# Mixer steps of a hybrid trunk: one place per unit of the dense stream instead of four

## The chip, the cores and the metric

The kernel runs on one core of a Trainium2 chip. The metric is the device time of one execution in microseconds, the median of several runs. Names of engines: TensorE (PE, with its weight loads PEld), VectorE (DVE), ScalarE (ACT), GpSimd (POOL) and SyncE (SP), which issues most of the DMAs.

## The reference

One pre-norm residual layer and a final norm on 256 tokens of width 2048, all in float32:

```python
D_MODEL = 2048; SEQ = 256; DEPTH = 1
h = rms_norm(x, norm_w)
p = h @ w_in                       # 2048 x 16592, one combined projection
qkv, z, b, a, feat, rz, su, sz, gates = split(p)
y0 = gated_delta_net(silu(conv4(qkv)), b, a) ; y0 = rms_norm(y0) * silu(z)   # 8 heads of 128, chunks
y1 = rwkv7(shift_mix(feat))                  ; y1 = (layer_norm(y1) + bonus) * silu(rz)  # 16 heads of 64
y2 = s5(su)                                  ; y2 = glu(gelu(y2)) * silu(sz) # 64 groups x 64 states
m  = sum(sigmoid(gates[i] + gate_b[i]) * (y[i] @ w_branch[i]) for i in range(3))
x  = x + m @ w_out
out = rms_norm(x, final_norm_w)
```

By far the largest part of the arithmetic is dense: w_in, w_branch, the glu weight and w_out. The three token mixers are many small matmuls with short elementwise chains between them.

## The kernel before

**The dense stream.** All dense work is one stream of *units*. A unit is 1024 columns' worth of weight, loaded by DMA as one 512 KB tile `raw` (four buffers), and split into a high part `whi` on ACT (L279) and a rest `wlo` on DVE (L280) two units ahead of its use (`load_unit`, called by `run_stream`). PE then does 24 matmuls of a full unit: for each of 8 slices of 128 rows high by high, high by low and low by high, into a bank of PSUM. A *job* is 128 output columns: 16 slices in two units for w_in, 8 slices in one unit for w_branch and the glu weight. When a job ends, `done` takes the result out of PSUM: a conv (ACT L665, then three DVE L667) for q, k, v of the delta net, a token shift (ACT L440, DVE L441) for r, k, v of the RWKV part, and a gate (`silu2`: ACT L684, DVE L685) for gz and rz. Two PSUM banks, `mm`, serve the dense jobs in turn; six, `br`, the mixers.

**The front** has eight rounds of eight jobs each (q, k, v, gz, r, k, v, rz), then gate jobs and the columns of S5. The tiles `gz` and `rz` have two buffers each, which become free again where the mixer's last step uses them: L821 for gz, behind the transposes `gp`, and the end of `rwkv_tail` for rz, behind the transposes `rq`. **The back** has the projections of the branches and the gates, with the S5 mixer beside it, the glu, and w_out.

**Mixer work** is written as generators. Each does a piece of work, a *step*, and yields how many calls of `pump` it wants to wait till its next one. They stand in queues called lanes: b (decays), g and r (the front parts of a delta-net head and an RWKV pair), t and i (the triangular inverses), g2 and r2 (their tails), s and sm (S5's tiles and S5's matrices). `pump()` counts each lane's `due` down and runs a step of those that are due. Before, it is called four times in a unit of eight slices: behind slices 1, 3 and 5 and after the unit, and a lane runs steps until it is no longer due.

**What sets the order.** PE's order is the program's: the class `InOrder` chains every matmul to the one before it. So a mixer matmul whose input isn't ready holds up the dense matmuls that are written behind it. The order on DVE, ACT and POOL comes from a scheduler that works from the program and the dependencies.

Names in the rows below: `gn` (norm sums of a head), `gp` and `rq` (the closing transposes of a head, of a pair), `ra`, `rc`, `rd`, `re` (RWKV state steps), `g` (delta-net tail), `ivp`/`ivZ` (the inverse on DVE, L548 and L550), `sm` (small columns: rsqrt chains at L121 to L137), `s5u`, `s5y` (S5 inputs and outputs of a tile), `s5wt`, `s5bt`, `s5ct` (its matrices).

Of the kernel before, what the change touches and what calls it, by code (L numbers as in the profile page):

```python
# [36 lines left out]
def tile_trunk(  # L37
# [1035 lines left out]
    lanes = {}  # L1073
    due = {}

    def lane(name, gen):
        lanes.setdefault(name, deque()).append(gen)

    def pump():
        for name in list(lanes):  # L1080
            due[name] = due.get(name, 0) - 1 if lanes[name] else 0
            while lanes[name] and due[name] <= 0:
                due[name] += step(name)

    def step(name):
        q = lanes[name]
        while q:
            try:
                return next(q[0])
            except StopIteration:  # L1090
                q.popleft()
        due[name] = 0
        return 0
# [11 lines left out]
    def mm_unit(u):  # L1105
        job = u["job"]
        if u["k0"] == 0:
            job["ps"] = [(br_bank if job["nps"] > 1 else mm_bank)(f"mm{un[0]}_{j}") for j in range(job["nps"])]
        kt, w, k0 = u["kt"], u["w"], u["k0"]
        last = k0 + kt == job["K"]  # L1110
        mh, ml = job["mov"]()
        if job["tok"]:

            job.setdefault("units", []).append(u)
            todo = [(0, u), (1, u)]
            if job["late"]:
                todo = [(0, u)] + [(1, v) for v in job["units"] if last]
            for a, v in todo:
                o = job["ps"][a]
                for k in range(kt):  # L1120
                    kk = v["k0"] + k
                    end = kk == job["K"] - 1
                    mhs, mls = mh[:, kk, a * P:(a + 1) * P], ml[:, kk, a * P:(a + 1) * P]
                    pe.matmul(o[:, 0:w], lhsT=mhs, rhs=v["hi"][:, k], start=kk == 0, stop=False)
                    pe.matmul(o[:, 0:w], lhsT=mhs, rhs=v["lo"][:, k], start=False, stop=False)
                    pe.matmul(o[:, 0:w], lhsT=mls, rhs=v["hi"][:, k], start=False, stop=end)
                if end:
                    job["done"](a, o)
        else:
            for k in range(kt):  # L1130
                kk = k0 + k
                if "pre" in job:
                    job["pre"](kk)
                for j, (c0, c1) in enumerate(job["cuts"]):
                    o = job["ps"][j][0:c1 - c0, 0:T]
                    pe.matmul(o, lhsT=u["hi"][:, k, c0:c1], rhs=mh[:, kk], start=kk == 0, stop=False)
                    pe.matmul(o, lhsT=u["hi"][:, k, c0:c1], rhs=ml[:, kk], start=False, stop=False)
                    pe.matmul(o, lhsT=u["lo"][:, k, c0:c1], rhs=mh[:, kk], start=False,
                              stop=last and k == kt - 1)
                if k % 2 and k < kt - 1:  # L1140
                    pump()
        if last and not job["tok"]:
            job["done"](job["ps"])
            if "after" in job:
                job["after"]()
# [36 lines left out]
    def run_stream(gen, ahead=2, q=()):  # L1182
        q = deque(q)
        gen = iter(gen)
        done = False
        while True:
            while not done and len(q) < ahead:
                try:
                    u = next(gen)
                except StopIteration:  # L1190
                    done = True
                    break
                load_unit(u)
                q.append(u)
            if not q:
                return
            mm_unit(q.popleft())
            pump()
# [528 lines left out]
```

## Time and profile before

| what | value |
|---|---|
| median of 3 runs | 1205.7 us (1205.07 to 1205.96) |
| profiled execution, its own time | 1205.63 us |
| its span in the profile | 1203.9 us |
| PE busy | 1181.4 us, 98% |
| DVE busy | 960.6 us, 80% |
| ACT busy | 621.1 us, 52% |
| HBM read | 195.88 MB |
| bytes moved over the span | 169 GB/s |

The time of an execution is a little more than the span, which goes from the first to the last record. Busy shares are averages over stages: the rounds of the front and their tails last to the last L821 at 614.5 us, S5's tiles fall into about 690 to 935 us, and the 260 us after that are dense work alone. Rows of groups read: line, engine, operation, output<-inputs, shape, count, then busy us and mean ns of one, then the idle time of the engine just ahead of them. Rows of the timeline read: start in us, length in us, engine, line, operation. A matmul of mixer data in float32 appears as two records.

### The profile page before, as it was taken

To read this page: it belongs to the slowest core of one execution; us is meant where nothing else is said; L and a number is where in the kernel's file an instruction comes from. 1 tells how busy PE (TensorE), PEld (TensorE's weight loads), DVE (VectorE), ACT (ScalarE), POOL (GpSimd) and SP (SyncE) were. 2 spreads that over 40 slices of the span, in tenths; PEclk is the share of its full clock that TensorE was granted. 3 is DMA by queue.
4 is the path that set the end of the run, shared out by engine and by line. 5 is a ranking of instruction groups with operands and counts; after the bars stand their busy time and mean duration, and the time that the engine had idled before them with its cause. 6 is when DMAs were issued, how large, how long until landed. Compare 5 with 4: busy or idle time off the path is not lost. (4 is left out here: it accounts for less than half of the span.)

```text
span 1203.9 us, 29305 instructions
## 1 busy us (share of the span) xinstructions
PE 1181.4 (98%) x11658; PEld 1127.5 (94%) x11658; DVE 960.6 (80%) x2515; ACT 621.1 (52%) x1190; POOL 62.9 (5%) x96
## 2 busy tenths in 40 slices
PE   5999999999999999999999999999999999999997
PEld 5999999999999999999999999999999999999886
DVE  7869888989899898977558988999998765555555
ACT  5455555556555656564544554444443554444443
POOL 4000000000000000000002011111100000000000
PEclk8999999999999999999999999999999999999999
DMA  5776655555555555555557677666767667677763
GB/s 167 196 192 156 167 129 157 138 150 144 136 150 141 146 145 147 134 141 142 158 163 194 191 193 185 184 183 187 195 170 196 171 181 189 179 190 238 240 197 115
DMA packets 384643, 203.98 MB, mean 169 GB/s; under 512 B 38825, under 2 KB 376186, under 8 KB 384122
## 3 DMA queue, kind: packets, MB, share of 16 engines
q1 hardware_dynamic: 382650, 199.61, 61.0%
q0 software_dynamic: 1536, 1.58, 0.5%
q8 instruction: 92, 1.51, 0.5%
q10 hardware_dynamic: 320, 0.93, 0.2%
q14 instruction: 45, 0.37, 0.1%
HBM read 195.88 MB, written 6.18 MB: 168 GB/s over the span
## 5 line engine op out<-in xcount | busy, mean ns | idle before, releaser
L62 PE MATMUL mm<-hT,whi 128*128 128x256 f32 (+1 forms) x4160 | 784.0, 289 | 4.2 <-DVE hT L247 3.5
L62 PEld LDWEIGHTS mm<-hT,whi 128*128 128x128 f32 (+1 forms) x4160 | 646.3, 191 | 17.8 <-DVE hT L247 4.3
L62 PE MATMUL mm<-hT,wlo 128*128 128x256 f32 (+1 forms) x2080 | 588.4, 283 | 0.4 <-DVE wlo L280 0.4
L279 ACT ACTIVATE whi<-raw 128x1024 fp32r<-128x1024 f32 (+1 forms) x346 | 364.6, 1055 | 361.1 <-PE mm L62 289.0
L280 DVE TENSOR_TENSOR wlo<-raw,whi 128x1024 fp32r<-128x1024 f32 (+1 forms) x345 | 422.2, 1224 | 151.0 <-ACT whi L279 149.2
L62 PEld LDWEIGHTS mm<-hT,wlo 128*128 128x128 f32 (+1 forms) x2080 | 397.4, 191 | 0.6 <-DVE wlo L280 0.6
L62 PE MATMUL mm<-oT,whi 128*128 128x256 f32 x768 | 140.4, 283 | 0.0
L62 PEld LDWEIGHTS mm<-oT,whi 128*128 128x128 f32 x768 | 118.9, 190 | 0.4 <-issue 0.4
L62 PE MATMUL mm<-oT,wlo 128*128 128x256 f32 x384 | 108.4, 282 | 0.0
L62 PE MATMUL mm<-whi,mT 128*128 128x512 f32 (+1 forms) x288 | 76.9, 354 | 0.0
L62 PEld LDWEIGHTS mm<-oT,wlo 128*128 128x128 f32 x384 | 73.2, 191 | 0.2 <-DVE wlo L280 0.2
L62 PEld LDWEIGHTS mm<-whi,mT 128*128 128x128 f32 x288 | 51.2, 189 | 7.5
L62 PE MATMUL mm<-wlo,mT 128*128 128x512 f32 (+1 forms) x144 | 50.9, 354 | 0.0
L548 DVE TENSOR_TENSOR ivp<-ivZ,ivX 48x1 f32<-48x1 f32 (+14 forms) x120 | 34.4, 287 | 1.4
L667 DVE SCALAR_TENSOR_TENSOR gc<-mm,pv,gc 128x255 f32<-128x255 f32 (+2 forms) x72 | 34.1, 473 | 0.9 <-ACT gc L665 0.3
L62 PEld LDWEIGHTS mm<-wlo,mT 128*128 128x128 f32 x144 | 27.2, 189 | 3.7
L550 DVE TENSOR_REDUCE ivZ<-ivp 48x1 f32<-48x1 f32 (+14 forms) x120 | 27.2, 227 | 1.5
L62 PE MATMUL mm<-ysp,whi 128*128 128x256 f32 x128 | 22.8, 281 | 0.0
L1220 DVE SCALAR_TENSOR_TENSOR gate<-gate,mm 128x256 f32<-128x256 f32 x32 | 13.4, 418 | 11.4 <-PE mm L62 11.4
L1210 ACT ACTIVATE gate<-mm,hgate 128x256 f32<-128x256 f32 x48 | 22.1, 461 | 0.3
L62 PEld LDWEIGHTS mm<-ysp,whi 128*128 128x128 f32 x128 | 19.6, 188 | 0.0
L670 ACT ACTIVATE gth<-gc 128x256 f32<-128x256 f32 x24 | 9.8, 410 | 16.6 <-DVE gc L667 15.1
(541 smaller groups left out, 1266.7 us busy)
## 6 DMA issues: line engine op xcount, KB each, us to landing
raw<-in_w_in_dram SPq DMA_DIRECT2D x256, 512.0 KB
raw<-in_w_branch_dram SPq DMA_DIRECT2D x48, 512.0 KB
raw<-in_w_out_dram SPq DMA_DIRECT2D x32, 512.0 KB
raw<-in_s_glu_w_dram SPq DMA_DIRECT2D x8, 512.0 KB
xs<-in_x_dram SPq DMA_DIRECT2D x4, 512.0 KB
xr<-in_x_dram SPq DMA_DIRECT2D x2, 1024.0 KB
raw<-in_w_in_dram SPq DMA_DIRECT2D x4, 384.0 KB
gr<-grow SPq DMA_DIRECT2D x8, 128.0 KB
```

Of the source, the lines that this page charges most:

```text
L62: return self.put(nc.tensor.matmul(*a, **k).ins)
L279: u["top"] = lambda: se.activation(out=hi[:, 0:nn], in_=raw[:, 0:nn], func=AF.Copy)
L280: u["sub"] = lambda eng=ve: eng.tensor_tensor(out=lo[:, 0:nn], in0=raw[:, 0:nn], in1=hi[:, 0:nn].bitcast(F32), op=ALU.subtract)
L548: ve.tensor_tensor(out=pi, in0=Z[:, 0:i, 0:i].rearrange("p j c -> p c j"), in1=X[:, i, 0:i].unsqueeze(1).to_broadcast([8 * NU, i, i]), op= ...
L550: ve.tensor_reduce(out=Z[:, i, 0:i], in_=pi, axis=AX.X, op=ALU.add)
L667: ve.scalar_tensor_tensor(out=c[:, s:T], in0=p[:, 0:T - s], scalar=pv("cw", (3 - s) * 24 + col), in1=c[:, s:T], op0=ALU.mult, op1=ALU.add)
L670: se.activation(out=th, in_=c, func=AF.Tanh, scale=0.5)
L1210: se.activation(out=t, in_=pss[0][:, 0:T], func=AF.Tanh, scale=0.5, bias=hgate[:, b * 16 + i:b * 16 + i + 1])
L1220: ve.scalar_tensor_tensor(out=g, in0=g, scalar=1.0, in1=p0, op0=ALU.add, op1=ALU.mult)
```

## The change

`pump()` is called only after a unit, no longer behind slices 1, 3 and 5. Each call takes 4 from `due`, so that the yields keep their meaning. A lane that is due does one step and then stops; a `due` below zero stays and lets the lane run a step at the next place too. The lanes s and sm still run steps until they are no longer due.

```diff
--- before.py
+++ after.py
@@ -1076,11 +1076,17 @@
     def lane(name, gen):
         lanes.setdefault(name, deque()).append(gen)
 
+    SLOT = 4
+    RUNS = ("s", "sm")
+
     def pump():
+
         for name in list(lanes):
-            due[name] = due.get(name, 0) - 1 if lanes[name] else 0
+            due[name] = due.get(name, 0) - SLOT if lanes[name] else 0
             while lanes[name] and due[name] <= 0:
                 due[name] += step(name)
+                if name not in RUNS:
+                    break
 
     def step(name):
         q = lanes[name]
@@ -1137,8 +1143,6 @@
                     pe.matmul(o, lhsT=u["hi"][:, k, c0:c1], rhs=ml[:, kk], start=False, stop=False)
                     pe.matmul(o, lhsT=u["lo"][:, k, c0:c1], rhs=mh[:, kk], start=False,
                               stop=last and k == kt - 1)
-                if k % 2 and k < kt - 1:
-                    pump()
         if last and not job["tok"]:
             job["done"](job["ps"])
             if "after" in job:
```

The number of instructions on each engine stays as it was. Dense matmuls on PE are interrupted by mixer matmuls at 162 places where there were 236. Lines behind the first hunk move by 6, those behind the second by 4.

PE, the closing transposes `gp` of head 1. Before, they stand alone in the midst of a unit (unit 60.5 counted in dense matmuls):

```order
L62 MATMUL mm_0_3534<-hT_75,whi_3441 128x256
L62 MATMUL mm_0_3534<-hT_76,whi_3441 128x256
L62 MATMUL mm_0_3534<-hT_75,wlo_3442 128x256
L65 MATMUL gp_3559<-ident,got_3308 128x128 x2
L62 MATMUL mm_0_3534<-hT_75,whi_3441 128x256
L62 MATMUL mm_0_3534<-hT_76,whi_3441 128x256
L62 MATMUL mm_0_3534<-hT_75,wlo_3442 128x256
```

With the change they come after unit 62, behind `gn` and `ra` of other lanes:

```order
L62 MATMUL mm_0_3519<-hT_75,wlo_3516 128x256
L62 MATMUL gn_3614<-ones,gsq_3488 128x1 x2
...
L62 MATMUL ra_3631<-rUV_3433,rg_3244 64x64
L62 MATMUL ra_3631<-rUV_3433,rg_3248 64x64
L65 MATMUL gp_3654<-ident,got_3308 128x128 x2
L62 MATMUL rd_3661<-rpn_2562,Mr_301 64x64 x2
L62 MATMUL mm_0_3672<-hT_75,whi_3581 128x256
L62 MATMUL mm_0_3672<-hT_76,whi_3581 128x256
```

`gn` and `ra`, which had places of their own before, now share one with `gp` and `rd`. On DVE the rows around this place, with the change:

```order
L131 SCALAR_TENSOR_TENSOR sm_3563<-sm_3559,sm_3556 128x1
L548 TENSOR_TENSOR ivp_3359<-ivZ_3353,ivX_3299 48x196
L131 SCALAR_TENSOR_TENSOR sm_3563<-sm_3559,sm_3556 128x1
L550 TENSOR_REDUCE ivZ_3353<-ivp_3359 48x14
L136 SCALAR_TENSOR_TENSOR sm_3564<-sm_3563 128x2
L722 COPY sm_3493<-gn_3614 128x2
L548 TENSOR_TENSOR ivp_3359<-ivZ_3353,ivX_3299 48x225
L137 SCALAR_TENSOR_TENSOR sm_3559<-sm_3564,sm_3559 128x2
L723 TENSOR_SCALAR sm_3493<-sm_3493 128x4
```

L722 reads the `gn` of this same place; the L137 that comes after it is the last row of the rsqrt for the scales of `got`, which `gp` transposes.

DVE, round 2, where the gz job's L685 takes its result out of its bank. Before:

```order
L992 TENSOR_TENSOR rpn_1637<-rc_2532,rpn_1637 128x64
L548 TENSOR_TENSOR ivp_2348<-ivZ_2342,ivX_2248 48x144
L730 SCALAR_TENSOR_TENSOR ges_2645<-gr_2476,gcol,posm 128x128
L550 TENSOR_REDUCE ivZ_2342<-ivp_2348 48x12
L821 SCALAR_TENSOR_TENSOR gog_2551<-gp_2548,hgnw,gz_802 128x256
L548 TENSOR_TENSOR ivp_2348<-ivZ_2342,ivX_2248 48x169
L685 SCALAR_TENSOR_TENSOR gz_2472<-zthgz_2473,mm_0_2324 128x256
L105 TENSOR_TENSOR oT_390<-gog_2551,oT_389 128x256
L550 TENSOR_REDUCE ivZ_2342<-ivp_2348 48x13
L280 TENSOR_TENSOR wlo_2605<-raw_2602,whi_2604 128x1024
```

L821 (`gog` of head 0) frees the buffer that L685 writes two rows on, with no split of L280 ahead of it here. With the change, first the rows up to the shift evacuation L441 behind unit 46, and then those up to L821 and L685:

```order
L722 COPY sm_2430<-gn_2536 128x2
L550 TENSOR_REDUCE ivZ_2297<-ivp_2303 48x13
L723 TENSOR_SCALAR sm_2430<-sm_2430 128x4
L548 TENSOR_TENSOR ivp_2303<-ivZ_2297,ivX_2250 48x196
L740 RECIPROCAL sm_2615<-sm_2430 128x2
L121 TENSOR_SCALAR sm_2618<-sm_2430 128x2
L550 TENSOR_REDUCE ivZ_2297<-ivp_2303 48x14
L122 TENSOR_SCALAR sm_2617<-sm_2618 128x2
L280 TENSOR_TENSOR wlo_2648<-raw_2645,whi_2647 128x1024
L548 TENSOR_TENSOR ivp_2303<-ivZ_2297,ivX_2250 48x225
L441 SCALAR_TENSOR_TENSOR scr<-mm_0_2459,pv_266,scr 128x255
```

```order
L992 TENSOR_TENSOR rpn_1646<-rc_2708,rpn_1646 128x64
L131 SCALAR_TENSOR_TENSOR sm_2696<-sm_2692,sm_2689 128x1 x2
L754 SCALAR_TENSOR_TENSOR gL_2677<-gg_2427,sm_2631,ges_2542 128x128
L136 SCALAR_TENSOR_TENSOR sm_2697<-sm_2696 128x2
L280 TENSOR_TENSOR wlo_2787<-raw_2784,whi_2786 128x1024
L441 SCALAR_TENSOR_TENSOR scr<-mm_0_2590,pv_266,scr 128x255
...
L280 TENSOR_TENSOR wlo_2874<-raw_2871,whi_2873 128x1024
L821 SCALAR_TENSOR_TENSOR gog_2775<-gp_2772,hgnw,gz_802 128x256
L999 COPY rUV_1477<-rd_2779 64x64
L685 SCALAR_TENSOR_TENSOR gz_2419<-zthgz_2420,mm_0_2316 128x256
```

The closing transposes of head 0 went from 45.25 units to 49; those of pair 0 (`rq`) from 51.25 to 55. L821 and L685 now come after two more evacuations of shift jobs (L441) and several splits (L280).

PE, an S5 tile. Before, the outputs of a tile and the matrix of the next stand together:

```order
L62 MATMUL mm_0_11346<-oT_390,whi_11304 128x256
L62 MATMUL mm_0_11346<-oT_389,wlo_11305 128x256
L62 MATMUL s5y_11372<-UM,WT_10992 32x256 x4
L62 MATMUL s5y_11372<-s5s_11336,CX_9908 32x64 x32
L62 MATMUL s5wt_11416<-CX_9909,B_9906 32x128 x8
L62 MATMUL mm_0_11440<-hT_75,whi_11342 128x256
L62 MATMUL mm_0_11440<-hT_76,whi_11342 128x256
```

With the change the matrix of the next tile comes first, one dense unit (24 matmuls) ahead of the outputs:

```order
L62 MATMUL mm_0_11374<-hT_75,wlo_11333 128x256
L62 MATMUL s5wt_11403<-CX_9909,B_9906 32x128 x8
L62 MATMUL mm_0_11374<-hT_75,whi_11370 128x256
...
L62 MATMUL mm_0_11374<-hT_75,wlo_11371 128x256
L62 MATMUL s5y_11453<-UM,WT_11030 32x256 x4
L62 MATMUL s5y_11453<-s5s_11399,CX_9908 32x64 x32
L62 MATMUL mm_0_11526<-oT_391,whi_11423 128x256
L62 MATMUL mm_0_11526<-oT_392,whi_11423 128x256
```

This parting holds in six of the seven tiles that have a next one.

## The prediction

> **What bounds the kernel now.** I read the totals of the page first, then what TensorE (PE) waits for, then the table of time windows. The page's totals and its dearest VectorE (DVE) line:
>
> ```profile
> span 1203.9 us, 29305 instructions
> PE 1181.4 (98%) x11658; PEld 1127.5 (94%) x11658; DVE 960.6 (80%) x2515; ACT 621.1 (52%) x1190; POOL 62.9 (5%) x96
> L280 DVE TENSOR_TENSOR wlo<-raw,whi 128x1024 fp32r<-128x1024 f32 (+1 forms) x345 | 422.2, 1224 | 151.0 <-ACT whi L279 149.2
> ```
>
> PE is busy 98% of the span. The view of PE's waits (total, times, longest) says where the rest is; the rows left out belong to the first 30 us, as the first one does, and to one wait of 0.2 us:
>
> ```profile
> PE nwp L65 <- DMA sc<-in_norm_w_dram: 3.9, 1, 3.9
> ...
> PE mm L62 <- ACT gate L1210: 0.5, 1, 0.5
> PE mm L62 <- DVE wlo L280: 0.4, 1, 0.4
> ```
>
> After the start PE waits about 1 us in all. So no wait is there to be removed: an edit that keeps all instructions and only places them anew can take at most about 1 us of waiting away, whatever it can put in. What it can put in depends on how much slack the other engines have where PE waits on them. The windows (PE, PEld, DVE, ACT, POOL busy, granted clock, DMA share, GB/s) of the start, of a stretch of the front, and of one tile of the S5 stage:
>
> ```profile
> core 0: us, PE busy (x) PEld busy (x) DVE busy (x) ACT busy (x) POOL busy (x), PEclk, DMA share, GB/s
> 0.00:30.00 30.00, 17.33 (x86) 15.41 (x86) 21.55 (x49) 17.47 (x32) 14.10 (x25) 0.83 0.59 167
> 400.00:500.00 100.00, 100.00 (x1035) 93.21 (x1034) 90.01 (x286) 58.18 (x135) 3.01 (x3) 1.00 0.53 138
> 748.50:775.80 27.30, 27.30 (x326) 26.59 (x326) 25.87 (x60) 13.00 (x26) 3.65 (x6) 1.00 0.72 186
> ```
>
> DVE is the second bound: 90.01 of 100 us in the front, 25.87 of 27.30 in an S5 tile. It runs its instructions in a fixed order, so a chain that PE needs also waits for whatever stands ahead of it there, above all the 1.22 us weight splits of L280. That is where I look for the price.
>
> **The change part by part.** Every instruction stays: PE's, DVE's, ACT's and the DMAs are the same in number. What moves is where the mixer steps stand between the dense matmuls: at most one step per lane after each whole unit, where before there were four places per unit. Three things follow: chains get longer where a lane needed several steps in one unit (lanes g2 and r2 fall behind in the early rounds), steps of several lanes share one place, and the DVE order around them is another one. PE's order is that of the program, so a step whose input is late stops all dense matmuls behind it.
>
> *A. The banks of the early rounds.* A dense job needs one of two "mm" banks. Before, the gz job of a round keeps its bank until the buffer that L685 writes is freed by L821, the end of the g2 lane of two rounds earlier:
>
> ```profile
> 172.42 0.37 ACT L684 ACTIVATE zthgz<-mm 128x256 f32<-128x256 f32 x1
> 177.15 0.48 DVE L821 SCALAR_TENSOR_TENSOR gog<-gp,hgnw,gz 128x256 f32<-128x256 f32 x1
> 177.91 0.40 DVE L685 SCALAR_TENSOR_TENSOR gz<-zthgz,mm 128x256 f32<-128x256 f32 x1
> 179.19 0.51 PE L62 MATMUL ra<-rUV,rg 64*64 64x64 f32 x10
> ```
>
> The bank is held from 172.42 to 178.31 and the next job that needs it begins behind the ra at 179.19: it fits by 0.9 us. In the changed order gp of that round stands 3.75 units later (after unit 49, was 45.25), and a unit is 24 matmuls at 0.12 us, 2.88 us (15.12 us for 126, row below in E). So the bank is missing for 10.8 us; both jobs that begin meanwhile (ends of units 46 and 48) take the bank of the job just ended and wait for its evacuation L441. The same holds for rz in that round (rq: 51.25 to 55), where the job that begins at the end of unit 54 waits for the three L667 of a conv job. The durations:
>
> ```profile
> 246.27 0.50 PE L62 MATMUL gn<-ones,gsq 128*128 128x1 f32 x4
> 243.15 0.68 PE L62 MATMUL ra<-rUV,rg 64*64 64x64 f32 x16
> 229.20 0.39 PE L62 MATMUL g<-gvn,gA 128*128 128x128 f32 x2
> 229.52 0.33 PE L62 MATMUL rd<-rpn,Mr 64*64 64x64 f32 x4
> 244.52 0.49 DVE L548 TENSOR_TENSOR ivp<-ivZ,ivX 48x196 f32<-48x196 f32 x1
> 244.93 0.47 DVE L441 SCALAR_TENSOR_TENSOR scr<-mm,pv,scr 128x255 f32<-128x255 f32 x1
> 245.85 0.55 DVE L548 TENSOR_TENSOR ivp<-ivZ,ivX 48x225 f32<-48x225 f32 x1
> 247.75 0.14 DVE L722 COPY sm<-gn 128x2 f32<-128x2 f32 x1
> 178.58 0.31 DVE L550 TENSOR_REDUCE ivZ<-ivp 48x13 f32<-48x169 f32 x1
> L992 DVE TENSOR_TENSOR rpn<-rc,rpn 128x64 f32<-128x64 f32 x24 | 5.2, 218 | 6.7 <-PE rc L62 6.7
> L131 DVE SCALAR_TENSOR_TENSOR sm<-sm,sm 128x1 f32<-128x1 f32 x72 | 13.7, 228 | 0.3
> L728 DVE SCALAR_TENSOR_TENSOR get<-gr,gcol,negm 128x128 f32<-128x128 f32 x16 | 5.4, 336 | 0.6 <-DMA gr<-grow 0.6
> ```
>
> (A four-byte mixer matmul has two records, so gn x4 is the two matmuls of one step.) First stall, end of unit 46: DVE stops at L722 for this place's gn, and then runs ten rows to the L441 that is waited for: L722, L723, L740, L121, L122 (0.15 each by L722, 0.75), L550 twice (0.31, 0.33), L548 twice (0.49, 0.55), one split (1.22) and L441 (0.47): 4.12, and gn ahead of it 0.50. Instructions of DVE begin about 0.07 before the record ahead ends (244.52 + 0.49 against 244.93), ten times 0.7: 3.9 us. PE itself has gn, ra (half of the sixteen shown; I take the whole as the bound that favours the change), g and rd to do, 0.50 + 0.68 + 0.39 + 0.33, less overlap 1.7. Stall 2.2. Second, end of unit 48: from rc (0.33) through L992 (0.22), two L131 (0.46), L754 (0.34, by L728, its like), L136 (0.15), a split (1.22) and L441 (0.47), 3.2, less overlap 0.4 and rc itself 0.3: 2.5. Third, end of unit 54, the conv evacuation:
>
> ```profile
> 227.87 0.46 ACT L665 ACTIVATE gc<-mm,pv 128x256 f32<-128x256 f32 x1
> 230.60 0.48 DVE L667 SCALAR_TENSOR_TENSOR gc<-mm,pv,gc 128x253 f32<-128x253 f32 x1
> ```
>
> From L665 to the end of the last L667 it takes 3.2 us, and in the changed order a split stands ahead of the first L667 at that point (1.1 of its 1.22 beyond L665): 4.3, with nothing of PE's to cover it. Sum of A: 9.0. Bounds: 4, if the splits have been done when the chain gets there (3 x 1.2 off, and the whole cover); 14, if two rows more stand in each way, or a fourth job meets a held bank.
>
> By the Trainium skill, page "TensorE: Matmul & The Clock Gate", section "Part 1: The HAM clock gate", a PE that idles for a window of about 3.4 us falls to half its clock and takes about as long to come back. The granted clock is 0.83 in the first 30 us, with the 3.9 us wait, and 1.00 in the other windows shown, so the trace does not speak against it. Only the third stall is long enough; at half clock for 3.4 us it would cost an estimated 1.7 us more, 1227.7 in place of the forecast below. The sum goes without it.
>
> *B. gp without its cover.* In rounds 1 to 6 gp now stands in the same place as gn and ra of other lanes (places 62, 78, 94, 110, 126, 142). The scales L815 that gp transposes come from the last L137 of a rsqrt, and on DVE that L137 now stands behind L722, which waits for this place's own gn, and a 48x225 L548. Before, there was a second between them:
>
> ```profile
> 236.38 0.68 ACT L815 ACTIVATE got<-got,sm 128x128 f32<-128x128 f32 x2
> 238.08 0.38 PE L65 MATMUL gp<-ident,got 128*128 128x128 f32 x2
> ```
>
> The scales ended at 237.06, gp began at 238.08. Now: gn 0.50, L722 0.14, L548 0.55, L137 0.15, two L815 0.68 make 2.0 us; PE has gn and ra of it, 1.1. Stall 0.9, with a hand-over between engines 1.0, six times: 6.0. Bounds: 0 (the scheduler's order lets L137 run before gn is there, when DVE is ahead) and 9 (0.5 more each, one more L550 in the way).
>
> *C. rq in the last place of the front* (round 7, after unit 164): its normalisation has one place less of cover; 0.7, between 0 and 2.
>
> *D. Splits in the S5 stage.* DVE has 27.30 - 25.87 = 1.4 us free in a tile of eight or nine units. Its work of a tile comes from s5u and s5y, which before could start at quarters of a unit and now at whole ones, so it is bunched: from s5y to the next s5u 2.0 units where there were up to 3.0. When such a bunch (some 5 us of s5m and CX work between splits) has to pass in one unit less, the next split is late. I take 0.4 us in each of the tiles, 3 in all; bounds 0 (as the one wait of 0.4 before) and 8 (one us in each of eight).
>
> *E. PE's own order.* 74 fewer places (236 to 162) at which PE goes from dense to small matmuls and back. What an interruption costs beyond the matmuls in it, from rows either side of it (between them lie two more dense matmuls, 3 x 0.12 us to be taken off):
>
> ```profile
> 717.41 0.28 PE L62 MATMUL mm<-hT,wlo 128*128 128x256 f32 x1
> 718.54 0.28 PE L62 MATMUL mm<-hT,wlo 128*128 128x256 f32 x1
> 933.27 0.28 PE L62 MATMUL mm<-hT,wlo 128*128 128x256 f32 x1
> 935.29 0.29 PE L62 MATMUL mm<-hT,wlo 128*128 128x256 f32 x1
> 825.97 0.28 PE L62 MATMUL mm<-hT,wlo 128*128 128x256 f32 x1
> 828.43 0.28 PE L62 MATMUL mm<-hT,wlo 128*128 128x256 f32 x1
> 838.41 15.12 PE mm L62 x126
> ```
>
> The first pair encloses s5wt alone: 1.13 - 0.36 = 0.77. The second s5y alone: 2.02 - 0.36 = 1.66. The third both together: 2.46 - 0.36 = 2.10. Together they save 0.33, and the change parts them in six of seven tiles: +2.0. The other mergers (gn with ra, rd with gp) are of small steps that I give 0.3 in all, so +1.7; bounds 0 and 3.
>
> Sum: 9.0 + 6.0 + 0.7 + 3.0 + 1.7 = 20.4. Against the profiled execution, 1205.63 (span 1203.9 and 1.7 around it; the median of the runs shown is 1205.7): 1226.0. All lower bounds give 1210, all upper ones 1242.
>
> **The rivals.** About 0.2% (2.4 us) is what a measurement of this kernel tells from no change.
>
> 1. *The new waits are hidden and only PE's order counts*: 1205.63 + 1.7 = 1207.3, no change. For it: a scheduler chooses the DVE order, and slack of 0.9 us (A) and 1.0 us (B) was there. Against: the delay of 10.8 us in A is far more than that slack, and PE's order cannot be changed by the scheduler. Chance 0.06.
>
> 2. *Faster*: PE gains from 74 fewer interruptions. At 0.1 us each (a third of the 0.33 above) it is -7.4, with nothing else: 1198. Against: the same rows show that what is saved is where large steps were joined, and the change parts those; waits would have to be zero as well. Chance 0.03.
>
> 3. *The S5 stage goes over to DVE*: if a tile's chain (s5u, s5m, CX, s5y) just misses a place and the next is a whole unit away, each tile is longer by what PE cannot fill. DVE has 1.4 us spare against 2.88 us for a unit: a loss of 1.5 to 2.9 in each of eight tiles, in place of D's 3. That gives 20.4 - 3 + 20 = 37: 1243. Against: dense work fills in between, since s5y does not stop it, and DVE's total stays. It decides when DVE's free time in a tile falls to nothing. Chance 0.07.
>
> **How the numbers follow.** The forecast 0.84, the rivals 0.06, 0.03 and 0.07. The forecast's own range is 1213 to 1237; to leave out no more than 2 in 10 and to take in part of the third rival I give 1211 to 1239. Faster by over 0.2%: the second rival and a little, 0.04. Within 0.2%: the first and the forecast's lowest edge, 0.06. Slower: 0.90.
>
> **What would show it.** The view of PE's waits must have rows that it lacks now: mm waiting for L441 twice and L667 once between 150 and 200 us, 2 to 4 us each (A); gp waiting for L815, six times near 1 us (B); mm waiting for L280, some 3 us in all after 690 us (D). PE's busy time should stay within 3 us of 1181.4 (E). If gp shows no wait, B is wrong; if the windows up to 250 us are not 8 us longer, A is. A shorter PE busy time by over 5 us would show the second rival, S5 tiles of 29 us or more the third.

## The result, and the profile after

The changed kernel takes 1235.1 us (median of 4 runs, 1234.4 to 1236.0) against 1205.75 us: 1.0245 times the time before, with a 95% interval of 1.0232 to 1.0259. It is slower by 29.4 us. The forecast was 1226.0 us (20.4 us slower) with a range of 1211 to 1239.

The totals of the changed kernel's page, then its view of what TensorE waits for (total, times, longest):

```profile
span 1234.0 us, 29256 instructions
PE 1192.7 (97%) x11658; PEld 1134.3 (92%) x11658; DVE 961.9 (78%) x2515; ACT 614.4 (50%) x1190; POOL 69.6 (6%) x96
```

```profile
PE gp L65 <- ACT got L815: 5.2, 6, 1.5
PE mm L62 <- DVE scr L441: 4.6, 2, 2.4
...
PE mm L62 <- ACT rk32h L859: 4.5, 1, 4.5
PE mm L62 <- DVE wlo L280: 4.2, 4, 2.0
```

These are waits that the kernel before did not have. Their number is the forecast one: two on L441, six on L815, some on L280, and one of 4.5 us. The page puts the last one down to L859, which ended at 224.23. No operand of that dense matmul comes from there; the conv evacuation that frees its bank ended at 224.11. The timeline of the changed kernel shows that evacuation, and where the waits fall (in brackets the idle time just ahead):

```profile
220.71 0.46 ACT L665 ACTIVATE gc<-mm,pv 128x256 f32<-128x256 f32 x1
220.83 1.23 DVE L280 TENSOR_TENSOR wlo<-raw,whi 128x1024 fp32r<-128x1024 f32 x1
221.98 0.48 DVE L667 SCALAR_TENSOR_TENSOR gc<-mm,pv,gc 128x255 f32<-128x255 f32 x1
...
223.63 0.48 DVE L667 SCALAR_TENSOR_TENSOR gc<-mm,pv,gc 128x253 f32<-128x253 f32 x1
```

```profile
181.43 0.58 PE L62 MATMUL mm<-hT,whi 128*128 128x256 f32 x1 [2.13 <-DVE scr L441]
193.38 0.39 PE L62 MATMUL mm<-hT,whi 128*128 128x256 f32 x1 [2.44 <-DVE scr L441]
224.25 0.36 PE L62 MATMUL mm<-hT,whi 128*128 128x256 f32 x1 [4.48 <-ACT rk32h L859]
259.46 0.33 PE L65 MATMUL gp<-ident,got 128*128 128x128 f32 x1 [0.73 <-ACT got L815]
582.04 0.33 PE L65 MATMUL gp<-ident,got 128*128 128x128 f32 x1 [1.50 <-ACT got L815]
```

The windows of round 2 (PE, PEld, DVE, ACT, POOL busy, granted clock, DMA share, GB/s) show both sides. First the kernel before, then the changed one:

```profile
core 0: us, PE busy (x) PEld busy (x) DVE busy (x) ACT busy (x) POOL busy (x), PEclk, DMA share, GB/s
150.00:200.00 50.00, 50.00 (x556) 46.80 (x555) 45.04 (x156) 28.52 (x70) 0.94 (x2) 1.00 0.53 138
200.00:250.00 50.00, 50.00 (x486) 46.61 (x484) 44.51 (x130) 28.15 (x63) 1.54 (x1) 1.00 0.55 142
```

```profile
150.00:200.00 50.00, 45.43 (x417) 42.52 (x416) 37.99 (x121) 23.36 (x53) 3.09 (x2) 0.90 0.50 127
200.00:250.00 50.00, 45.52 (x489) 42.36 (x489) 38.36 (x110) 25.33 (x64) 0.73 (x1) 0.97 0.46 119
```

PE lost 9 us of these 100 to waiting, as forecast. The clock column shows what was not in the sum: 0.90 and 0.97 where it was 1.00. Shorter windows right behind four of the waits:

```profile
181.40:187.20 5.80, 5.77 (x26) 5.62 (x26) 2.42 (x15) 0.41 (x1) 0.00 (x0) 0.50 0.45 107
195.00:197.60 2.60, 2.60 (x14) 2.60 (x14) 0.00 (x0) 0.00 (x0) 0.18 (x1) 0.52 0.55 150
225.00:228.30 3.30, 3.30 (x17) 3.30 (x17) 1.88 (x10) 0.00 (x0) 0.03 (x1) 0.51 0.07 22
583.40:586.70 3.30, 3.30 (x17) 3.30 (x17) 0.47 (x2) 0.23 (x1) 0.00 (x0) 0.51 0.78 179
```

Behind these waits PE runs at half clock, for 3.4 us or twice 3.4.

To see where the 29.4 us arise, each dense matmul's start is compared in the two traces; both have 8064 in the same order, so the difference at any point is the delay up to there. It is 0.3 us at unit 40, 15.6 at unit 56, 20.3 at unit 136, 23.9 at unit 184 (the last ahead of the S5 tiles) and 30.1 from unit 256 on. Split by kind:

| term | forecast | measured | how read |
|---|---|---|---|
| A, three waits of round 2 | 9.0 | 9.05 | 2.13 + 2.44 + 4.48 |
| B, gp waiting for L815 | 6.0 | 5.2 | five times 0.73, once 1.50 |
| C, rq | 0.7 | 0.4 | 0.08, 0.12, 0.18 |
| D, splits in the S5 stage | 3.0 | 3.4 | 4.3 of waits less the 0.9 that were there before |
| half clock behind waits | 0 | 7.0 | 3.4 us five times, about 1.4 lost each (below) |
| E, PE's own order | 1.7 | 4.9 | the rest of 30.0, which is 30.1 less the 0.1 there at unit 0 |

### The profile page after: what moved, and what is told of

The parts are those of the page before. It is cut to its first block, busy times and chain, and to the rows that moved or that the text cites. A ratio compares the mean times of both kernels' runs of the same rounds, so it can differ in the third digit from the quotient of the medians.

```text
span 1234.0 us, 29256 instructions
## 1 busy us (share of the span) xinstructions
PE 1192.7 (97%) x11658; PEld 1134.3 (92%) x11658; DVE 961.9 (78%) x2515; ACT 614.4 (50%) x1190; POOL 69.6 (6%) x96
## 4 chain that ended last, share of the span: by engine, by line
PE 89%; DVE 6%; ACT 2%; issue 1%; DMA 1%; SPq 0%; DVEq 0%; ACTq 0%
PE mm L62 78%; DVE wlo L280 2%; ACT whi L279 1%; PE s5y L62 1%; PE rg L62 1%; PE rd L62 1%; PE g L62 1%; PE ryo L62 1%; DMA xs<-in_x_dram 1%; PE re L62 1%; PE gg L62 1%; PE rw L62 0%; PE rc L62 0%; PE s5wt L62 0%; PE ivy L62 0%
## 5 line engine op out<-in xcount | busy, mean ns | idle before, releaser
L280 DVE TENSOR_TENSOR wlo<-raw,whi 128x1024 fp32r<-128x1024 f32 (+1 forms) x345 | 422.2, 1224 | 167.9 <-ACT whi L279 163.5
L548 DVE TENSOR_TENSOR ivp<-ivZ,ivX 48x1 f32<-48x1 f32 (+14 forms) x120 | 34.3, 286 | 1.7
L667 DVE SCALAR_TENSOR_TENSOR gc<-mm,pv,gc 128x255 f32<-128x255 f32 (+2 forms) x72 | 34.4, 477 | 0.5
L62 PE MATMUL mm<-ysp,wlo 128*128 128x256 f32 x64 | 18.0, 281 | 0.0
```

The lines of the kernel that those rows point to most:

```text
L62: return self.put(nc.tensor.matmul(*a, **k).ins)
L280: u["sub"] = lambda eng=ve: eng.tensor_tensor(out=lo[:, 0:nn], in0=raw[:, 0:nn], in1=hi[:, 0:nn].bitcast(F32), op=ALU.subtract)
L548: ve.tensor_tensor(out=pi, in0=Z[:, 0:i, 0:i].rearrange("p j c -> p c j"), in1=X[:, i, 0:i].unsqueeze(1).to_broadcast([8 * NU, i, i]), op= ...
L667: ve.scalar_tensor_tensor(out=c[:, s:T], in0=p[:, 0:T - s], scalar=pv("cw", (3 - s) * 24 + col), in1=c[:, s:T], op0=ALU.mult, op1=ALU.add)
```

## The experiments

Shares of the delay are given as above, by the stream position. "Front" is the delay gained from unit 40 to 184, "S5" from 184 to 256; in the changed kernel 23.5 and 6.2.

**The two stages apart.** The order of places is switched where the front ends (this fence and the next two are shown against the changed kernel, with parts left out):

```diff
...
-            due[name] = due.get(name, 0) - SLOT if lanes[name] else 0
+            due[name] = due.get(name, 0) - (4 if new[0] else 1) if lanes[name] else 0
...
-                if name not in RUNS:
+                if new[0] and name not in RUNS:
...
+                if not new[0] and k % 2 and k < kt - 1:
+                    pump()
...
     finish("g", "r", "t", "i", "g2", "r2")
+    new[0] = False      # or: False ahead of here, True from here on
```

> The changed places in the front alone (up to the end of the rounds and their tails); the S5 stage and all behind it with four places per unit as before. By unit of the dense stream the changed kernel's trace stands 23.8 us behind the one before at unit 184, the last one ahead of the S5 tiles, so if front and S5 stage pay apart this run takes 1205.7 + 23.8 = 1229.5 us, with the waits on L441 (two), on the conv evacuation (one) and on L815 (six) all there. Rival: the lateness of the front is partly what makes S5 slow, or is partly caught up in S5's waits; then this run and the one with the change in the S5 stage alone do not add up to +29.4 us (they would miss it by 3 us or more).

> The changed places from the S5 stage on, the front with four places per unit as before. If the two parts pay apart: 30.1 - 23.9 = 6.2 us of drift between units 184 and 256 in the changed kernel's trace, so 1211.9 us, made up of waits on L280 (some 3.4 us more than before) and of PE's own order (about 2.9 us). Rival: S5 alone is hidden, 1206 to 1208 us, because the splits are late only after the delay of the front.

The S5 stage alone: 1212.0 us (1.0051, interval 1.0034 to 1.0068), as expected to 0.1 us. The kernel's view of PE's waits has nothing new but this:

```profile
PE mm L62 <- DVE wlo L280: 4.0, 4, 1.6
```

So S5 pays 6 us by itself, without the late front. The front alone: 1227.1 us, 2.4 less than expected; its four executions lie apart (1224.8, 1225.3, 1228.9, 1229.1). In the profiled one, of 1224.8 us, all waits of the changed kernel's front are there and of the same length (2.13, 2.44, 4.48, 0.73 five times; 1.31 in place of 1.50), but only two stretches of 3.4 us at half clock in place of the five of the changed kernel. The delay of the front is 19.3 in place of 23.5 us: of the 4.2 us between them 0.2 are wait, and three stretches make the rest, so one costs about 1.3 us by this; the single one behind the wait of 1.50 in the changed kernel added 1.48 between units 142 and 143, against the same stretch of this run. The parts add up: 21.3 + 6.2 = 27.5 of 29.4, the difference being within what the clock makes of equal waits.

**Is it the bank?** A third buffer for gz, or for rz:

```diff
-                t = ft([P, T], tag, f"{tag}{i0 + j}", bufs=2)
+                t = ft([P, T], tag, f"{tag}{i0 + j}", bufs=3 if tag == "gz" else 2)   # or "rz"
...
-    NG = 9
+    NG = 8
```

> The changed kernel with a third buffer for the gz tiles (one gate tile less makes the room, so one gate job moves from the front to the back). If the bank that the gz job holds is the cause, the waits of 2.13 and 2.44 us on L441 go, and with them the two stretches at half clock that follow (6.8 and 3.4 us, 5.1 us lost): 1235.1 - 9.7 = 1225.4 us; the third wait (4.48 us, round 2's conv) stays with its own stretch at half clock. Rival: DVE's lateness is the cause, not the bank; then the waits go over to another release and the time stays at 1233 us or more. Rival on the clock: the half-clock stretches are not due to the waits and stay: 1230.5 us.

> The changed kernel with a third buffer for the rz tiles in place of gz's. If the bank of the rz job is the cause of the third wait, the 4.48 us go and the stretch at half clock behind it (3.4 us, 1.7 lost): 1235.1 - 6.2 = 1228.9 us; the two waits on L441 stay with their own stretches. Rival: the wait stays in another place (another release for the same matmul), 1233 us or more.

Both got slower than the changed kernel: 1244.2 us and 1240.1 us, 1.0322 and 1.0285 times the kernel before. Some 6 us of that have nothing to do with the banks: with one gate job fewer in the front, the first S5 transposes come before their DMA has landed (a wait of about 2.9 us, another of 0.7 and two windows at half clock). At unit 152, ahead of those transposes, the delay is 23.6 us in the changed kernel, 24.0 with gz's buffer and 23.2 with rz's: up to there neither has gained anything to speak of. What matters is round 2. With gz's third buffer the two waits on L441 are gone, and this stands in their place, first of round 2, then of round 3:

```profile
193.31 0.33 PE L65 MATMUL gp<-ident,got 128*128 128x128 f32 x1 [3.55 <-ACT got L815]
257.20 0.33 PE L65 MATMUL gp<-ident,got 128*128 128x128 f32 x1 [1.47 <-ACT got L815]
```

With rz's third buffer the conv wait is gone, and rq waits instead, for longer. The rows of VectorE ahead of it, some left out:

```profile
222.08 1.22 DVE L280 TENSOR_TENSOR wlo<-raw,whi 128x1024 fp32r<-128x1024 f32 x1
...
224.17 1.21 DVE L280 TENSOR_TENSOR wlo<-raw,whi 128x1024 fp32r<-128x1024 f32 x1
225.31 0.15 DVE L137 SCALAR_TENSOR_TENSOR sm<-sm,sm 128x4 f32<-128x4 f32 x1
...
226.31 0.85 DVE L1044 TENSOR_SCALAR ryn<-ryo,rmv,sm 128x64 f32<-128x64 f32 x3
226.96 0.47 PE L65 MATMUL rq<-ident,ryn 128*128 128x128 f32 x1 [5.18 <-DVE ryn L1044]
```

gz's buffer did shorten round 2, by 3 us up to unit 56, but gp then waits 1.46 or 1.47 us in each of the next five rounds, where the changed kernel has 0.73. The bank is where the wait showed, not what it was worth. While PE stood at the bank, VectorE worked off what gp and rq need next; with the bank free, PE goes on and stops at gp or rq. The tails' steps are late on VectorE by about as much either way.

**Is it the debt of the tails?** g2 and r2 with the old places and all else changed, and the reverse:

```diff
...
+    TAILS = ("g2", "r2")
...
-    def pump():
+    def pump(mid=False):
         for name in list(lanes):
-            due[name] = due.get(name, 0) - SLOT if lanes[name] else 0
+            fine = (name in TAILS) == True      # or False
+            if mid and not fine:
+                continue
+            due[name] = due.get(name, 0) - (1 if fine else 4) if lanes[name] else 0
             while lanes[name] and due[name] <= 0:
                 due[name] += step(name)
-                if name not in RUNS:
+                if not fine and name not in RUNS:
                     break
...
+                if k % 2 and k < kt - 1:
+                    pump(True)
```

> The changed kernel, but the two lanes that fall into debt, g2 and r2, keep the four places per unit and the old rule; all other lanes and the S5 stage as changed. gp of head 0 then stands at unit 46.25 (45.25 before, 49 changed), rq of pair 0 at 52.25 (51.25, 55), and gp no longer shares its place with gn. If the debt of the tails is what the front pays for: the L441 waits shrink to one of about 2 us (gp is one unit later than before), the conv wait and the L815 waits go, S5's 6.2 us stay: 1205.8 + 6.2 + 2 + 1 = 1215 us. Rival: what counts is that DVE gets the other lanes' work in bunches; then most of the front's 21 us stays, 1225 us or more.

> The reverse: only the lanes g2 and r2 get one place per unit and one step there, all other lanes and S5 as before. gp of head 0 stands at unit 48, rq of pair 0 at 54, gp stands with rd alone, not with gn and ra. If the debt of the tails is the cause: the bank of the gz job is missing at the end of units 46 and perhaps 48, that of rz at 54; waits of 5 to 9 us in all with two or three stretches at half clock (1.7 us each) and about 0.5 us for each of six gp: 1216 to 1223 us. Rival: bunching of the other lanes is the cause; then below 1211 us.

1234.4 us (1.0240) and 1238.6 us (1.0269): both as slow as the whole change, or slower. The debt theory falls. Its rival, the bunching of the other lanes, is met by the first time (1225 or more) and missed by the second (below 1211), so it does not explain both either. With the tails back at four places the waits of round 2 are indeed nearly gone (one of 1.08 us is left on L441), and gp has 0.45 us where it had 0.73, but other steps wait, in nearly every round:

```profile
PE re L62 <- DVE rUV L999: 5.7, 5, 1.3
PE g L62 <- ACT gvn L799: 4.4, 7, 0.7
...
PE gp L65 <- ACT got L815: 2.3, 5, 0.5
```

The front's delay is 22.7 us, spread evenly (3.7 per round from round 3 on, of it 2.4 waits). Of the 22.7 us, 15.0 are waits; No stretch at half clock follows these shorter waits, so 7.7 are left for PE's own order, more than in the changed kernel. In the reverse case it is again L441, in five rounds more than before, and rq:

```profile
PE mm L62 <- DVE scr L441: 10.0, 7, 1.7
...
PE rq L65 <- DVE ryn L1044: 4.3, 3, 4.0
```

(Some 5 us of the reverse case's time, beyond its front, are again S5's first transposes, which come before their DMA.) So three different assignments of places cost the front about 23 to 29 us, half clock included, through different waits.

**gp one place later:**

```diff
-        yield 6
+        yield 18 if h else 6
         pq = br_bank(f"gp{h}")
```

> The changed kernel, with the closing transposes gp of heads 1 to 7 one place later (the norm's yield is 18 in place of 6, which the debt does not eat). If the wait of gp for L815 is that its scales have too little time, 0.73 us five times and 1.50 once go (5.2 us), and with the longest one a stretch at half clock (1.7 us): 1228 to 1230 us; the three waits of round 2 stay. Rival: gp later holds the gz bank longer, and a wait on L441 comes up in every round: 1235 us or more. Since two executions of a kernel with such waits have differed by 4 us in the time, the waits in the trace decide, more than the median.

1229.7 us (1.0203; 1229.5 to 1230.7), in the expected range; no wait on L815 is left. But the rival's wait came too. PE's view has three waits on L441 more than the changed kernel, and two put down to L733 in the same place of their rounds; the five are 1.17 to 1.18 us long, one in each of rounds 3 to 7 (rounds counted from 0):

```profile
PE mm L62 <- DVE scr L441: 8.1, 5, 2.4
...
PE mm L62 <- DVE sm L733: 2.3, 2, 1.2
```

In those rounds the gain is 0.15 us each. What was really given back is the longest wait with its stretch at half clock, 3.7 us between units 136 and 144, and one stretch in round 2 by chance.

**Half the change**, two places per unit:

```diff
-    SLOT = 4
+    SLOT = 2
...
+                if k == 3 and kt == 8:
+                    pump()
```

> The changed kernel with two places per unit (behind slice 3 and after the unit, 2 taken off each time), still one step per lane and place. gp of head 0 comes at 47.5 and rq of pair 0 at 53.5. If the price comes from single late steps, which half a unit of lead mostly covers: one wait on L441 of about 2 us, gp waits under 0.3, S5 about half its price: 1214 us (1209 to 1219). Rival: the price goes with the number of places taken away (the change takes two of four in place of three of four): about two thirds of 29.4 us, 1225 us.

1220.0 us (1.0118), between the two expectations: front 11.0, S5 1.2 us. The wait on L441 that was expected is not there; gp waits 2.0 us once and 0.46 five times instead. Its waits are many and short; PE's view has 4.3 us on L815, 2.0 on L999 and 1.1 on L1010, and no half clock followed any of them. Nearly half of the front's price, with two of three removed places still removed, and almost none of S5's: half a unit of lead covers much, not all.

**The clock.** Thirteen waits of chosen length, in the dense stretch of the kernel before, without and with 24 small matmuls ahead (the function that holds these lines is left out):

```diff
...
+        for k in range(0):      # or 24
+            pe.matmul(p[0:64, 64:128], lhsT=ident[0:64, 0:64], rhs=ident[0:64, 0:64], start=True, stop=True)
+        for k in range(2):
+            pe.matmul(p[:, k:k + 1], lhsT=ident, rhs=ones, start=True, stop=True)
+        ve.tensor_copy(c, p[:, 0:2])
+        ge.tensor_tensor(out=a[:, 0:2], in0=a[:, 0:2], in1=c, op=ALU.mult)
+        for k in range(i % 7):
+            ge.tensor_tensor(out=a[:, 0:W_], in0=a[:, 0:W_], in1=a[:, 0:W_], op=ALU.mult)
+        pe.matmul(p[:, 2:3], lhsT=ident, rhs=a[:, 0:1], start=True, stop=True)
```

> The kernel before, with thirteen waits put into the dense stretch behind the S5 stage, one every four units (11.5 us): one small pair of matmuls, a copy on VectorE, a chain of 1 to 7 multiplies of 128x128 on GpSimd, and a small matmul that waits for it. Nothing else changes. In the changed kernel the clock was halved behind waits of 2.13, 2.44, 4.48 and 1.50 us, not behind those of 0.73, 1.52 and 1.95 us. If a window of about 3.4 us that is no more than about half busy is enough (the stretches at half clock are 3.4 us or twice that), waits from about 2 us up are followed by half clock, some by chance and some not, since the window's start is not tied to the wait; a wait under 1.5 us never is. By the Trainium skill, page TensorE: Matmul & The Clock Gate, section Part 1: The HAM clock gate, it takes an idle window of about 3.4 us: then only waits of over 3.4 us are. The time is that of before, 1205.8 us, plus the waits (each as the trace shows it), plus 1.7 us for each stretch of 3.4 us at half clock.

> The same thirteen waits, each with 24 small matmuls (64x64, about 1 us) ahead of it. If small matmuls count as idle for the clock gate, half clock follows waits that are shorter by about 1 us than in the run without them (from about 1 us up). If they count as work, it follows the same lengths of wait as there.

The two runs took 1268.8 and 1314.1 us, one execution each. The first is 8 us above the waits (38.2 us) and ten stretches of 3.4 us at 1.7 each; the few small matmuls beside each wait, which the expectation left out, lengthen the time between dense matmuls by some 0.7 us beyond the wait. Without the 24 small matmuls, the waits of 0.59 to 2.80 us (five) left the clock at 1.00, and those of 2.89 to 4.66 us (eight) each brought half clock. The timeline of the two nearest to each other:

```profile
962.53 0.27 PE L62 MATMUL q<-qa,ident 128*128 128x1 f32 x1 [2.80 <-POOL qa L1661]
1090.54 0.27 PE L62 MATMUL q<-qa,ident 128*128 128x1 f32 x1 [2.89 <-POOL qa L1661]
```

The windows behind them, columns as above:

```profile
962.60:966.00 3.40, 3.40 (x29) 3.40 (x30) 1.01 (x3) 0.59 (x2) 0.31 (x1) 1.00 0.54 154
1090.90:1093.90 3.00, 3.00 (x16) 3.00 (x16) 0.00 (x0) 0.00 (x0) 0.31 (x1) 0.50 0.65 179
```

With the 24 small matmuls ahead, which took 2.8 us and not the expected 1, all thirteen were followed by half clock, the shortest wait too. Its row in the timeline, then the windows of the small matmuls and behind them:

```profile
1071.24 0.27 PE L62 MATMUL q<-qa,ident 128*128 128x1 f32 x1 [0.59 <-POOL qa L1659]
```

```profile
1066.90:1071.30 4.40, 3.81 (x56) 3.52 (x54) 1.39 (x2) 1.06 (x1) 0.20 (x1) 1.00 0.61 155
1071.70:1074.70 3.00, 3.00 (x15) 3.00 (x16) 0.00 (x0) 0.00 (x0) 0.31 (x1) 0.50 0.30 91
```

PE is "busy" for 3.81 of those 4.40 us and loses its clock nevertheless. So small matmuls do not count as work here, and what counts is the time between two dense matmuls. The shortest in this run is 4.5 us, so it says nothing on how small matmuls and waits compare below that. Over the traces of before, the changed kernel and the runs told so far, by that time (start to start, less the 0.12 us of a dense matmul):

| dense to dense | followed by half clock |
|---|---|
| 1.0 to 2.4 us | 2 of 597 |
| 2.4 to 2.8 us | 4 of 26 |
| 2.8 to 3.6 us | 7 of 14 |
| 3.6 to 4.0 us | 3 of 5 |
| over 4.0 us | 29 of 29 |

Between 2.4 and 4.0 us the same gap can go either way: the 3.9 us at unit 46 stands in four traces with the changed front, and half clock follows in two. That would explain why the front alone varied by 4 us, since eight of its gaps lie in that range, three of them above 2.8; it is not shown, for only one execution of each kernel has a trace. The mean granted clocks of the executions agree for rz's third buffer (1237.0 and 1237.8 us at 0.990 and 0.991, 1242.4 and 1243.1 us at 0.982 and 0.981), but do not sort the four of the front alone (0.989 to 0.991). By the Trainium skill, page "TensorE: Matmul & The Clock Gate", section "Part 1: The HAM clock gate", it takes an idle window of about 3.4 us, and the window runs freely. The stretches of 3.4 us and the chance between 2.4 and 4.0 agree with a free window of that length; that it has to be idle does not: a window with a 0.59 us wait in it was enough, and in the changed kernel one of 1.50.

**Is VectorE's queue the cause?** Every second split of the front and the S5 stage on GpSimd, PE's order unchanged:

```diff
-            u["sub"]()
+            u["sub"](ge if 30 <= i < 260 and i % 2 else ve)
```

> The changed kernel, with every second weight split L280 of units 30 to 259 on GpSimd in place of VectorE (115 of 345; 1.22 us each on VectorE, about 2.4 us each on GpSimd by the one 832-wide row of 1.94 us). PE's order stays word for word. If the waits of the changed kernel come from steps that queue on VectorE behind splits and other rows, they shrink: the two L441 waits and the conv wait from 9.0 to about 5 us, the L815 waits and the S5 waits on L280 nearly gone, with one or two stretches at half clock left: 1218 us (1213 to 1223). Rival: the chains' own hand-overs between engines are what PE waits for, not the queue; then the waits stay and the time is 1230 us or more. A third way: GpSimd is too slow or disturbs VectorE; then PE waits for wlo from GpSimd, and the time is over 1240 us.

> The same splits on GpSimd in the kernel before. It has no waits of note, so if GpSimd does no harm it stays within 1204 to 1208 us; if GpSimd's splits are late or slow VectorE down, it gets slower, and that is what the run with the changed kernel pays too.

1335.5 us (1.1074), and the kernel before with it 1312.0 us (1.0881): the third way by the time. PE's waits, however, are on VectorE's own splits (26.1 us in ten waits) and hardly on GpSimd's (1.0 us in one): GpSimd disturbs VectorE. Groups of the changed kernel with GpSimd's splits, then L667 and L548 of the changed kernel without:

```profile
L280 POOL TENSOR_TENSOR wlo<-raw,whi 128x1024 fp32r<-128x1024 f32 (+1 forms) x116 | 286.2, 2467 | 580.9 <-ACT whi L279 438.5 <-DVE sm L136 33.2 <-DVE rpn L992 29.8
...
L548 DVE TENSOR_TENSOR ivp<-ivZ,ivX 48x1 f32<-48x1 f32 (+14 forms) x120 | 50.9, 424 | 2.4
L667 DVE SCALAR_TENSOR_TENSOR gc<-mm,pv,gc 128x255 f32<-128x255 f32 (+2 forms) x72 | 34.3, 477 | 13.3 <-ACT gc L665 12.4
```

```profile
L667 DVE SCALAR_TENSOR_TENSOR gc<-mm,pv,gc 128x255 f32<-128x255 f32 (+2 forms) x72 | 34.4, 477 | 0.5
L548 DVE TENSOR_TENSOR ivp<-ivZ,ivX 48x1 f32<-48x1 f32 (+14 forms) x120 | 34.3, 286 | 1.7
```

A split takes 2.47 us on GpSimd, and VectorE's own L548 goes from 286 to 424 ns. L667, which reads PSUM, keeps its length of 477 ns. By the Trainium skill, page "SBUF — State Buffer", section "SBUF: two separate sides", GpSimd and an operation of VectorE with both inputs in SBUF exclude each other for a whole instruction, and the later one stands still; the rows agree: L548 is of that kind, L667 is not. The 16 L548 that overlap a split on GpSimd are 1.03 us longer on average than in the changed kernel, the other 104 not at all. The kernel before gets 106 us slower with the same edit, so the run says nothing on the changed kernel's waits. That VectorE's queue is the cause is therefore not shown by taking load away. What speaks for it are windows of the changed kernel around the gp waits, where VectorE has no idle time at all while PE waits 0.73 us:

```profile
255.00:260.00 5.00, 4.27 (x46) 3.85 (x44) 5.00 (x25) 3.15 (x8) 0.00 (x0) 1.00 0.39 105
320.00:325.00 5.00, 4.27 (x48) 3.77 (x46) 5.00 (x23) 3.15 (x9) 0.00 (x0) 1.00 0.39 111
```

## Why the prediction was right

**What bounds the kernel** held: there was nothing to gain, and all that happened is new waits and PE's own order. VectorE as the second bound is where nearly all the large waits end: in L441, L667, the rsqrt ahead of L815, L280, L999, L1044.

**A** named the three waits, their places by unit and their lengths: 2.2, 2.5 and 4.3 forecast, 2.13, 2.44 and 4.48 measured. (The overlap of "ten times 0.7" is a slip of the pen for 0.07, and the sum goes by 0.07. The third wait falls at 224 us, not between 150 and 200.) The sum of rows from the place where VectorE stops, less what PE still has to do, was the right way to price a wait: the rows that were added up for the first one are those that ran, from L722 at 178.04 to the end of L441 at 181.37. What the part said on the cause is only half right. The bank decides which matmul waits, but not how much is lost: without the bank's hold, gp waited 3.55 us in place of 2.13 + 2.44, and rq 5.18 in place of 4.48.

**B** was right in place and number, 5.2 for 6.0, but not in all of its steps. In five of the six places the rows are like these, of unit 62, others between them left out:

```profile
257.62 0.50 PE L62 MATMUL gn<-ones,gsq 128*128 128x1 f32 x4
258.06 0.14 DVE L136 SCALAR_TENSOR_TENSOR sm<-sm 128x2 f32<-128x2 f32 x1
258.15 0.16 DVE L722 COPY sm<-gn 128x2 f32<-128x2 f32 x1
258.66 0.46 ACT L440 ACTIVATE scr<-mm,omu 128x256 f32<-128x256 f32 x1
258.68 0.15 DVE L137 SCALAR_TENSOR_TENSOR sm<-sm,sm 128x2 f32<-128x2 f32 x1
259.01 0.68 ACT L815 ACTIVATE got<-got,sm 128x128 f32<-128x128 f32 x2
```

L722 follows L136 without a gap, at the moment when gn ends (258.12). So VectorE did not stand still for gn, as the sum has it; its own rows ran out just then, and that both come together is luck. L815 then begins 0.18 us after L137 ends, with ScalarE in L440 of the shift job until 259.12, a step that the part does not have. In the sixth place, the longest wait (1.50 us), no gn stands at all: the scales are held by VectorE's rows alone. That gp is paid by itself is wrong in the same manner: given one place more, it no longer waits, and a dense matmul behind it waits for L441 for 1.17 us.

**C and D** were right within 0.5 us in their sums. D's sum is not spread as forecast, 0.4 us in each tile: two waits, of 1.52 and 1.95 us, make 3.5 of the 4.3. Ahead of the first of them VectorE is full, mostly with s5m and CX work, from the end of one split at 842.62 to the start of the next at 847.21, the bunch that the part names. The S5 stage alone confirms D and S5's part of E: 6.2 us in 1212.0.

**E failed in its size and its bound**: 4.9 in place of 1.7, above the 3 that was its upper end. The parted s5y and s5wt, six times 0.33, account for 2.0 of S5's 2.9; the 0.3 in all for the other mergers was no measurement, and some 3 us are left for them, as the rest of a sum and not measured apart. PE's busy time rose by 11.3 us, to 1192.7, where the prediction allowed 3: half clock (7.0) and E (4.9) make about that.

**The clock is the term that was missing.** The sum went without it, and the sentence beside it let only the third wait be long enough, for 1.7 us. Five windows at half clock, 7.0 us, came behind waits of 2.13, 2.44, 4.48 and 1.50. The first wait lay in a place of small matmuls, 3.9 us from dense to dense. With the clock the sum is 20.4 + 7.0 = 27.4; E's excess of 3.2, D's of 0.4, and B's and C's shortfall of 1.1 make the rest of 30.0. That 1235.1 still lies between 1211 and 1239 is owed to a range that was drawn wide for other reasons.

**The rivals.** That the waits are hidden and that PE gains from fewer interruptions are both refuted by PE's view and its busy time. The third, S5 as VectorE's bound with 1243 us, did not happen: S5 paid 6.2 us, and the end lay above the forecast for the reason of the clock.

What stays open is why every other spacing of the front that was tried costs 11 to 29 us. Three assignments of places give different waits and about the same sum, and VectorE is full around the waits that were looked at; whether a lighter VectorE would hide them could not be tried with GpSimd.

## What to carry to other kernels

Where one engine is at 98% and a second at 90% in a fixed order, the spacing of the small steps matters, and here each other spacing that was tried was slower: price a new spacing wait by wait, from the row at which the second engine stops. A wait removed by a buffer is not yet a gain; look for the next step that needs the same late work before counting it. And add to each place of small matmuls the time from dense to dense: over 4 us it brought half clock each time, 1.3 us or more, and between 2.4 and 4 us some of the time.

## What was not expected of the hardware

Small matmuls did not keep the clock up: 54 records in 4.4 us with only 0.59 us of wait ended in half clock, thirteen times of thirteen. With equal waits, the number of half-clock windows differed between executions (five and two in the same front), and four executions of one kernel lay 4.3 us apart, of another 6.1, where the kernel before, with no such gaps, stays within 2.

A split of 128x1024 on GpSimd took 2.47 us against 1.22 on VectorE, and with 116 of them VectorE's small multiplies L548 became 1.5 times as long (286 to 424 ns, 287 to 528 in the kernel before with the same edit).
